# A hybrid decoder's step on one core: two requests' paged values summed on VectorE, the recurrence's outer products formed on TensorE

## The chip, the cores and the metric

One core of a Trainium2 chip runs the whole program. Its engines work side by side, each on its own queue of instructions in order: TensorE (PE) multiplies matrices, VectorE (DVE) and ScalarE (ACT) work elementwise, GpSimd (POOL) does a little elementwise work and issues transfers, SyncE (SP) only issues transfers. Sixteen DMA engines carry these between HBM and the core's SBUF; TensorE writes to PSUM. The metric is the time of one execution on the device, in us.

## The reference, cut to what matters

One layer of a decoder is computed for a prompt of 512 tokens and for eight sample requests with one token each. The mixer has two halves: a gated linear recurrence (HGRN2) and differential attention over a paged cache of 4096 positions per request. Memory cross-attention and a SwiGLU FFN follow. Two pieces of the samples' work are touched here:

```python
# recurrence, per request b and head h (one token): S is 128 x 128
S_new = f[:, None] * S + k[:, None] * v[None, :]
o     = S_new.T @ q
# differential attention over 32 pages of 128 positions, per request
k_past = cache_k[page_table]                 # 32 pages x 128 x 4 heads x 128
v_past = cache_v[page_table]
p = softmax(q . k)                           # two maps
w = p[map 0] - lam * p[map 1]
o = sum over positions of w[position] * v_past[position]      # per head
```

## The kernel before, in words

All data is float32. The prompt's matrix products dominate: each weight row block `raw` of 128 rows is split into a rounded part `hi` (ScalarE, `round_weights`, L655) and a remainder `lo` (VectorE, `remainders`, L669), and each output block takes three products (`block`, L696). A *row of weights* below is one such `hi`/`lo` pair: 12 products of 128x128 by 128x512 in most blocks. `hi` and `lo` lie in rings of three buffers, the raw weights in three of two rows each, all loaded by SyncE (`load_weights`, L617).

The samples' work runs between. `load_keys` and `load_values` (L1099) fetch pages through `stream` (L934), a ring of six buffers of two pages (512 KB), with `gather` (L942) reading page numbers and issuing a DMA per page on SyncE. `sum_values` (L1109) takes, for each request, 32 pages in four visits of eight: each page is multiplied on TensorE by a 128x32 matrix of weights `wt`, four pages side by side in the four groups of 32 columns, accumulated in the PSUM tile `pv`. `value_out` (L1130) then selects each head's row through `pvsel` into `po` and VectorE adds it to `oda_s`.

`sample_recurrence` (L1474) goes through the eight requests: GpSimd loads the state `st`, and loads the request's value row `v` from a copy in HBM (`spill`, `load_row`, L569 to L577) to all 128 partitions as `kv`; ScalarE scales each head's block of `kv` by `k`; VectorE forms `st = f * st + kv`; GpSimd stores it; TensorE multiplies by `q`. GpSimd's queue, in order, holds these triples and other stores.

The order of all instructions is fixed when the program is built. Every piece of work is a generator with a rank; `Weave.run` (L312) always advances the best-ranked one that a model clock (`Clock`, L134) deems ready, and some streams may run VectorE or ScalarE only `LEAD` ahead of TensorE. `pace` (L954) gives a stream its rank only as far as it is behind a straight line over rows of weights: keys over rows 10 to 80 (`KPACE`), values over rows 80 to 150 (`VPACE`). What comes after the samples' attention (`load_rest`, L1872, projections, cross-attention) starts when the values are done; blocks of the FFN that the prompt has passed before the samples reach them are fetched apart (`s_ffn_alone`, L2048). Because every instruction is recorded in `Timed` (L295), all have the line L305 in the profile, and the names of tiles tell them apart.

Of the kernel before, what the change touches and what calls it, by code (L numbers as in the profile page):

```python
# [12 lines left out]
F32 = mybir.dt.float32  # L13
# [365 lines left out]
def decode_step(ctx: ExitStack, tc: tile.TileContext, io: dict):  # L379
# [29 lines left out]
    def slot(s, shape=(P, T), dt=F32):  # L409
        return fp.tile(list(shape), dt, tag="slot", bufs=SLOTS, name=nm(s))  # L410
# [52 lines left out]
    def rsmall(shape, s):  # L463
        return small(shape, s, "r", 2)
# [4 lines left out]
    def row(s):  # L469
        return ring(sp, [P, T], "row", 2, s)  # L470

    def mm(out, a, b, start, stop):
        pe.matmul(out, lhsT=a, rhs=b, start=start, stop=stop)
# [92 lines left out]
        use(pt[:, :P].rearrange("p (g b) -> p g b", b=32))  # L566
        at_give()

    def spill(q, name):  # L569

        d = dp.tile([P, P], F32, name=name)
        pool.dma_start(d, q)
        return d.rearrange("(g b) c -> b g c", b=32)

    def load_row(dst, d, b):

        pool.dma_start(dst.rearrange("p (g c) -> p g c", g=4), d[b].partition_broadcast(P))  # L577


    sizes = [512] * (DFF // 512)  # L580
    sizes.insert(SMALL, DFF % 512)
# [352 lines left out]
    def stream(name):  # L934

        n = streamed[0]
        streamed[0] += 1
        yield lambda: n - KBUFS < done["keys"] + 2 * done["values"] + len(spent) + 2 * done["cmv"] + done["proj"]
        yield clock.next("stream", KBUFS)
        return ring(kp, [P, KPG, T], "stream", KBUFS, name)  # L940

    def gather(which, at, dst):  # L942

        for i, t in enumerate(dst, at):
            if i % PBATCH == 0:
                _, pages[which] = real.values_load_multi_w_load_instructions(
                    ptab[:, which == "cache_v", i : i + PBATCH], [mybir.EngineType.SP], min_val=0, max_val=n_phys - 1,
                    skip_runtime_bounds_check_because="the numbers are clamped to the cache on the chip",
                )
                clock.free["sp"] += 0.53 + 0.03 * PBATCH  # L950
            page = pages[which][i % PBATCH]
# [72 lines left out]
    def sample_softmax():  # L1024
# [71 lines left out]
        dve.tensor_copy(by_quad(wnew), w32.rearrange("p (x b y) -> p x b y", x=2, y=2))  # L1096
        S["wnew"] = True

    def load_values():  # L1099

        yield lambda: len(kts) == NB * nst
        for n in range(NB * NCH):
            pair = []
            for _ in range(2):
                pair.append((yield from stream("cache_v")))
            vts[n] = [t[:, i, :] for t in pair for i in range(KPG)]
            gather("cache_v", 4 * n, vts[n])

    def sum_values():  # L1109
        for n in range(0, NB * NCH, LUMP // 2):  # L1110
            b, s0 = divmod(n, NCH)
            yield lambda: n + LUMP // 2 - 1 in vts and done["soft"] == NB
            if s0 == 0:
                yield from pv_room()
                acc = pvt("pv")
            yield (*(t for i in range(LUMP // 2) for t in vts[n + i]), wts[s0 // 2])
            for s in range(s0, s0 + LUMP // 2):
                w = wts[s // 2].rearrange("p (j b c) -> p j b c", j=2, b=NB)[:, s % 2, b, :]
                for i in range(4):
                    mm(acc[32 * i : 32 * i + 32, :], w, vts[n + s - s0][i], s == 0, s == NCH - 1)  # L1120
            done["values"] = n + LUMP // 2
            if s == NCH - 1:
                yield (acc,)
                pvs = row("pvs")
                act.copy(pvs, acc)
                pv_give()
                weave.add(value_out(b, pvs), 3, "t")
                yield lambda: done["out"] >= b - 1

    def value_out(b, pvs):  # L1130
        yield lambda: done["out"] == b
        yield (pvs,)
        yield from at_room()
        po = att("po")
        for h in range(4):
            mm(po[32 * h : 32 * h + 32, :P], pvsel[:, h, 7 - b : 39 - b], pvs[:, h * P : (h + 1) * P], True, True)
        yield (po,)
        if b == 0:
# [4 lines left out]
        done["out"] = b + 1  # L1143
        if b == NB - 1:
            give(4)
            S["da"] = True

# [326 lines left out]
    def sample_recurrence(sqT, sfT, svq, sgT):  # L1474
        skT = keep([P, 4, 8], "skT")
        lb3 = lb.unsqueeze(2).to_broadcast([P, 4, 8])
        om3 = omlb.unsqueeze(2).to_broadcast([P, 4, 8])
        sig = rsmall([P, 4, 8], "sig")
        yield from sigmoid(sig, skT, sfT)
        dve.scalar_tensor_tensor(skT, skT, BIG, sig, op0=ALU.min, op1=ALU.mult)  # L1480
        dve.tensor_tensor(skT, skT, om3, op=ALU.mult)
        dve.tensor_tensor(sig, sig, om3, op=ALU.mult)
        dve.tensor_tensor(sfT, sig, lb3, op=ALU.add)
        yield
        sig2 = rsmall([P, 4, 8], "sig")
        yield from sigmoid(sig2, sig2, sgT)
        dve.tensor_mul(sgT, sgT, sig2)
        vd = spill(svq, "vd")
        yield from room(2)
        for b in range(NB):  # L1490
            st = slot("st")
            pool.dma_start(st, io["state"][b])
            kv = slot("kv")
# [12 lines left out]
            yield  # L1506
            for h in range(HEADS):
                sl = slice(h * P, (h + 1) * P)
                dve.scalar_tensor_tensor(
                    st[:, sl], st[:, sl], sfT[:, h, b : b + 1], kv[:, sl], op0=ALU.mult, op1=ALU.add  # L1510
                )
            yield
# [359 lines left out]
    def load_rest():  # L1872


        yield lambda: len(vts) == NB * NCH
        yield lambda: "mix" in S or done["values"] >= NB * NCH - LUMP
# [218 lines left out]
    def sample_query(hs):  # L2095
# [20 lines left out]
        yield from new_scores()  # L2116
        S["sn"] = True
        yield lambda: V_FROM in raws
        weave.add(sum_values(), pace(VRANK, "values", NB * NCH, VPACE))
        weave.add(load_values(), 1)  # L2120

    def follower():
# [490 lines left out]
```

## Time and profile before

| | |
|---|---|
| time, median of 3 runs | 1142.68 us (1138.63 to 1144.46) |
| the profiled execution | 1134.85 us, its span 1133.1 us |
| TensorE, share of the span | 95% |
| VectorE | 48% |
| ScalarE | 38% |
| GpSimd | 6% |
| bytes by DMA | 279.75 MB, mean 247 GB/s |

Shares are averages over stages with different limits: the recurrence, keys and the prompt's attention up to some 420 us, the values from 447 to 704 us, the FFN after that. The page's chain of waits names what ended last; a stretch view gives every engine's busy time, the clock granted to TensorE, and the busy share and rate of the DMA engines for that part alone.

### The profile page before, as it was taken

To read this page: it belongs to the slowest core of one execution; us is meant where nothing else is said; L and a number is where in the kernel's file an instruction comes from. 1 tells how busy PE (TensorE), PEld (TensorE's weight loads), DVE (VectorE), ACT (ScalarE), POOL (GpSimd) and SP (SyncE) were. 2 spreads that over 40 slices of the span, in tenths; PEclk is the share of its full clock that TensorE was granted. 3 is DMA by queue.
4 is the path that set the end of the run, shared out by engine and by line. 5 is a ranking of instruction groups with operands and counts; after the bars stand their busy time and mean duration, and the time that the engine had idled before them with its cause. 6 is when DMAs were issued, how large, how long until landed. Compare 5 with 4: busy or idle time off the path is not lost.

```text
span 1133.1 us, 23098 instructions
## 1 busy us (share of the span) xinstructions
PE 1072.3 (95%) x8846; PEld 777.3 (69%) x8846; DVE 546.1 (48%) x1126; ACT 428.3 (38%) x915; POOL 70.4 (6%) x97
## 2 busy tenths in 40 slices
PE   8999799987987889899999999999999999999997
PEld 6777587865665557466666666776577677777776
DVE  6743777534654654444443443453343333443535
ACT  6413443436454556333444332341232221222333
POOL 0000010213101110000300000000000000000002
PEclk9999899988998989999999999999999999999999
DMA  7979665998999995999998799579978982234102
GB/s 255 352 242 324 206 215 174 291 253 259 319 308 278 274 304 169 309 329 332 319 338 285 241 325 343 201 244 359 344 266 291 351 305 75 63 89 129 38 1 75
DMA packets 143376, 279.75 MB, mean 247 GB/s; under 512 B 15281, under 2 KB 20529, under 8 KB 143266
## 3 DMA queue, kind: packets, MB, share of 16 engines
q1 hardware_dynamic: 137970, 264.13, 67.8%
q0 software_dynamic: 4064, 13.05, 6.1%
q8 instruction: 69, 1.13, 0.4%
q10 hardware_dynamic: 1232, 1.11, 0.3%
q14 instruction: 41, 0.34, 0.1%
HBM read 269.35 MB, written 8.88 MB: 246 GB/s over the span
## 4 chain that ended last, share of the span: by engine, by line
PE 81%; DMA 10%; DVE 3%; issue 3%; ACT 1%; SPq 1%; POOL 0%; DVEq 0%; POOLq 0%; ACTq 0%
PE mm L305 56%; DMA cache_k<-cache_k 6%; PE pv L305 5%; PE ks L305 4%; PE sgu L305 2%; PE cs L305 2%; PE sdn L305 1%; DMA kv<-vd 1%; PE ss L305 1%; PE co L305 1%; PE sgm L305 1%; PE pd L305 1%; PE sacc L305 1%; PE oda L305 1%; PE cpv L305 1%
## 5 line engine op out<-in xcount | busy, mean ns | idle before, releaser
L305 DVE TENSOR_TENSOR lo<-raw,hi 128x512 fp32r<-128x512 f32 (+1 forms) x260 | 176.6, 681 | 434.2 <-ACT hi L305 406.1
L305 PE MATMUL mm<-sh,hi 128*128 128x512 f32 (+1 forms) x832 | 339.8, 408 | 4.2 <-ACT sh L305 3.9
L305 ACT CAST hi<-raw 128x512 fp32r<-128x512 f32 (+1 forms) x260 | 157.5, 607 | 490.5 <-PE mm L305 443.3
L305 PE MATMUL mm<-sl,hi 128*128 128x512 f32 (+1 forms) x832 | 324.1, 390 | 0.8 <-DVE sl L305 0.8
L305 PE MATMUL mm<-sh,lo 128*128 128x512 f32 (+1 forms) x832 | 323.0, 388 | 0.0
L305 PEld LDWEIGHTS mm<-sh,hi 128*128 128x128 f32 x832 | 157.2, 189 | 78.6 <-issue 39.0
L305 PEld LDWEIGHTS mm<-sh,lo 128*128 128x128 f32 x832 | 157.5, 189 | 34.0 <-DVE lo L305 0.4
L305 PEld LDWEIGHTS mm<-sl,hi 128*128 128x128 f32 x832 | 157.8, 190 | 28.9 <-DVE sl L305 1.4
L305 PE MATMUL ks<-cache_k,qst 128*32 128x128 f32 x2048 | 72.3, 285 | 16.1 <-DMA cache_k<-cache_k 16.0
L305 PEld LDWEIGHTS ks<-cache_k,qst 128*32 128x32 f32 x2048 | 57.6, 114 | 32.7 <-DMA cache_k<-cache_k 24.0
L305 PE MATMUL pv<-cache_v,wt 128*32 128x512 f32 x512 | 63.4, 608 | 0.0
L305 PE MATMUL mm<-hi,sh 128*128 128x512 f32 x128 | 54.5, 426 | 0.0
L305 PE MATMUL mm<-lo,sh 128*128 128x512 f32 x128 | 50.5, 395 | 0.0
L305 PE MATMUL mm<-hi,sl 128*128 128x512 f32 x128 | 50.5, 394 | 0.0
L305 DVE TENSOR_TENSOR res<-mm,res 128x512 f32<-128x512 f32 (+1 forms) x68 | 42.2, 652 | 9.2 <-PE mm L305 9.2
L305 PEld LDWEIGHTS pv<-cache_v,wt 128*32 128x32 f32 x512 | 14.5, 110 | 31.1 <-issue 22.1
L305 DVE SCALAR_TENSOR_TENSOR lo<-raw,par,hi 128x512 fp32r<-128x512 f32 x16 | 13.2, 826 | 35.1 <-ACT hi L305 35.1
L305 PEld LDWEIGHTS mm<-hi,sh 128*128 128x128 f32 x128 | 24.3, 190 | 7.9 <-issue 3.1
L305 PE MATMUL mm<-hi,mh 128*128 128x512 f32 x64 | 28.5, 446 | 0.9 <-ACT hi L305 0.9
L305 PEld LDWEIGHTS mm<-hi,sl 128*128 128x128 f32 x128 | 24.3, 190 | 5.5
L305 PEld LDWEIGHTS mm<-lo,sh 128*128 128x128 f32 x128 | 24.4, 191 | 4.5 <-issue 0.5
L305 PE MATMUL mm<-lo,mh 128*128 128x512 f32 x64 | 25.2, 394 | 0.2 <-DVE lo L305 0.2
(419 smaller groups left out, 1210.3 us busy)
## 6 DMA issues: line engine op xcount, KB each, us to landing
cache_k<-cache_k SPq DMA_DIRECT2D x256, 256.0 KB, 5.6
cache_v<-cache_v SPq DMA_DIRECT2D x256, 256.0 KB, 4.8
raw<-w_in SPq DMA_DIRECT2D x27, 512.0 KB, 5.1
raw<-w_down SPq DMA_DIRECT2D x22, 512.0 KB, 4.2
raw<-w_gate SPq DMA_DIRECT2D x20, 512.0 KB, 5.0
raw<-w_up SPq DMA_DIRECT2D x20, 512.0 KB, 4.5
cache_mem_k<-cache_mem_k SPq DMA_DIRECT2D x16, 512.0 KB, 6.2
cache_mem_v<-cache_mem_v SPq DMA_DIRECT2D x16, 512.0 KB, 7.4
```

Of the source, the lines that this page charges most:

```text
L305: ins = getattr(self.engine, op)(*a, **k)
```

## The change

Requests 3 and 7 (`BY_DVE`) have their values summed on VectorE: the softmax weights of a request are gathered in `wm` with one column per page and head, and for each page and head one instruction adds value times weight, per position (partition), to an accumulator `va` (128 x 512). Its sum over the 128 positions is then formed by `value_out` with a selection of ones (`ohrow`). The value tiles come in a new order (`vorder`): three of the six other requests' tiles, then one of these. `summed` counts a tile as done only when all before it in that order are, and that count feeds the ring. The values' pace is stretched to rows 80 to 170.

In the recurrence, `k` is transposed once to rows (`krows`); a row mask (`mine`) leaves, for request b, its four heads' rows (`km`); `vcols` holds each head's `v` in its own columns and rows, zero elsewhere. One product `km` by `vcols` in plain fp32 gives the four heads' outer products in PSUM, which VectorE reads as `kv`. The copy of `v` in HBM and the eight loads of it are gone.

```diff
+BY_DVE = (3, 7)
+EVERY = 3
-VPACE = (80, 150)
+VPACE = (80, 170)
...
-        yield lambda: n - KBUFS < done["keys"] + 2 * done["values"] + len(spent) + 2 * done["cmv"] + done["proj"]
+        yield lambda: n - KBUFS < done["keys"] + done["values"] + len(spent) + 2 * done["cmv"] + done["proj"]
...
+    while by_pe or by_dve:
+        vorder += by_pe[:EVERY] + by_dve[:1]
+        del by_pe[:EVERY], by_dve[:1]
...
     def sum_values():
...
+        if BY_DVE:
+            weave.add(sum_values_dve(), 5, "d")
+        for b in range(NB):
+            if b in BY_DVE:
+                continue
...
+    def sum_values_dve():
...
+            acc = slot("va")
+            for s in range(nst):
+                yield lambda: b * nst + s in vts
+                v = vts[b * nst + s]
+                yield tuple(v)
+                for i in range(KPG):
+                    for h in range(HEADS):
+                        c = slice(h * P, (h + 1) * P)
+                        k = 4 * (KPG * s + i) + h
+                        if s + i == 0:
+                            dve.tensor_scalar(acc[:, c], v[i][:, c], wm[:, k : k + 1], None, op0=ALU.mult)
+                        else:
+                            dve.scalar_tensor_tensor(
+                                acc[:, c], v[i][:, c], wm[:, k : k + 1], acc[:, c], op0=ALU.mult, op1=ALU.add
+                            )
+                    yield 0.0
+                summed(b * nst + s)
...
-        vd = spill(svq, "vd")
         yield from room(2)
...
+        yield from s_tr(padded, lambda pt: dve.tensor_copy(krows, pt.rearrange("p g b -> p (g b)")))
+        for h in range(HEADS):
+            r = slice(32 * h, 32 * h + 32)
+            act.copy(vcols[r, h * P : (h + 1) * P], svq[r])
...
-            load_row(kv, vd, b)
-            yield
-            for h in range(HEADS):
-                sl = slice(h * P, (h + 1) * P)
-                act.activation(kv[:, sl], kv[:, sl], AF.Copy, scale=skT[:, h, b : b + 1])
+            km = quadt("km")
+            dve.tensor_scalar(km, krows, mine[:, b : b + 1], None, op0=ALU.mult)
...
+            yield from at_room()
+            kv = att("kv")
+            mm(kv, km, vcols, True, True)
+            yield (kv, st)
```

On TensorE, at the recurrence's first request, the program before goes on like this (`mm` is a block of the prompt's projections, `so` the state times `q`, `ks` the scores of eight pages of keys):

```order
L305 MATMUL mm_3068<-sl_202,hi_3306 128x512
L305 MATMUL mm_3068<-sh_201,lo_3340 128x512
L305 MATMUL so_3423<-st_3268,qm_3386 32x128 x4
L305 MATMUL mm_3136<-sh_201,hi_3306 128x512
L305 MATMUL mm_3136<-sl_202,hi_3306 128x512
L305 MATMUL mm_3136<-sh_201,lo_3340 128x512
L305 MATMUL mm_3147<-sh_201,hi_3306 128x512
L305 MATMUL mm_3147<-sl_202,hi_3306 128x512
L305 MATMUL mm_3147<-sh_201,lo_3340 128x512
L305 MATMUL ks_3416<-cache_k_3193,qst_588 32x128 x8
L305 MATMUL ks_3416<-cache_k_3230,qst_588 32x128 x8
L305 MATMUL ks_3416<-cache_k_3344,qst_588 32x128 x8
```

In the changed program the same place reads:

```order
L307 MATMUL mm_3136<-sl_202,hi_3315 128x512
L307 MATMUL mm_3136<-sh_201,lo_3349 128x512
L307 MATMUL ks_3421<-cache_k_3193,qst_588 32x128 x8
L307 MATMUL ks_3421<-cache_k_3230,qst_588 32x128 x8
L307 MATMUL ks_3421<-cache_k_3353,qst_588 32x128 x8
L307 MATMUL ks_3421<-cache_k_3356,qst_588 32x128 x8
L307 MATMUL kv_3490<-vcols_3267,km_3381 128x512
L307 MATMUL mm_3147<-sh_201,hi_3315 128x512
L307 MATMUL mm_3147<-sl_202,hi_3315 128x512
L307 MATMUL mm_3147<-sh_201,lo_3349 128x512
L307 MATMUL mm_3257<-sh_201,hi_3315 128x512
L307 MATMUL mm_3257<-sl_202,hi_3315 128x512
```

One product `kv` stands behind the keys' scores, and `so` of that request comes 12 products of the prompt later.

On VectorE, at the prompt's memory queries (`cq`, `cql`) and the splits of memory values and keys (`mvl`, `kl`), the program before has:

```order
L305 SCALAR_TENSOR_TENSOR lo_6879<-raw_6657,par,hi_6841 128x512
L305 TENSOR_TENSOR cq_6885<-mm_6550,rbc 128x512
L305 TENSOR_TENSOR cql_6867<-cq_6829,cqh_6866 128x512
L305 TENSOR_TENSOR mvl_6870<-mv_5163,mvh_6869 128x512
L305 SCALAR_TENSOR_TENSOR lo_6908<-raw_6657,par,hi_6898 128x512
L305 TENSOR_TENSOR kl_6873<-mkT_4511,kh_6872 128x512
L305 TENSOR_TENSOR kl_6888<-mkT_4513,kh_6887 128x512
L305 TENSOR_TENSOR cql_6911<-cq_6885,cqh_6910 128x512
L305 TENSOR_TENSOR mvl_6903<-mv_5202,mvh_6902 128x512
L305 TENSOR_TENSOR mvl_6941<-mv_5791,mvh_6940 128x512
L305 TENSOR_TENSOR mvl_6989<-mv_5802,mvh_6988 128x512
L305 TENSOR_REDUCE cmx_6948<-cs_6947 128x2
```

The changed program has there:

```order
L307 SCALAR_TENSOR_TENSOR lo_6957<-raw_6742,par,hi_6945 128x512
L307 TENSOR_TENSOR mvl_6937<-mv_5710,mvh_6936 128x512
L307 TENSOR_TENSOR cql_6952<-cq_6893,cqh_6951 128x512
L307 SCALAR_TENSOR_TENSOR va_5965<-cache_v_6919,wm_5960,va_5965 128x128 x8
L307 SCALAR_TENSOR_TENSOR lo_6999<-raw_6793,par,hi_6975 128x512
L307 TENSOR_TENSOR cql_6963<-cq_6902,cqh_6962 128x512
L307 TENSOR_TENSOR mvl_6979<-mv_5922,mvh_6978 128x512
L307 TENSOR_TENSOR oda_s<-oda_s,po_6981 128x128
L307 TENSOR_REDUCE cmx_7007<-cs_7006 128x2
L307 TENSOR_SCALAR cmx_7007<-cmx_7007 128x2
L307 SCALAR_TENSOR_TENSOR lo_7047<-raw_6793,par,hi_7037 128x512
L307 TENSOR_TENSOR mvl_7023<-mv_5955,mvh_7022 128x512
```

Eight sums of one value tile (two pages, four heads) stand between two remainders `lo`, in a queue that otherwise holds the same kinds of instructions.

## Rows read from the trace of the kernel before

**Rows 1.** The page's head: span, busy time of each engine.
```profile
span 1133.1 us, 23098 instructions
PE 1072.3 (95%) x8846; PEld 777.3 (69%) x8846; DVE 546.1 (48%) x1126; ACT 428.3 (38%) x915; POOL 70.4 (6%) x97
```

**Rows 2.** Stretches: length, busy us, granted clock, DMA share, GB/s.
```profile
0.00:220.00 220.00, 203.91 (x2926) 162.70 (x2927) 139.65 (x320) 92.17 (x205) 17.52 (x31) 0.96 0.77 259
220.00:420.00 200.00, 169.92 (x1702) 121.63 (x1701) 103.12 (x249) 96.74 (x237) 34.15 (x46) 0.92 0.96 281
300.00:320.00 20.00, 18.92 (x215) 14.47 (x214) 13.18 (x37) 10.02 (x25) 2.89 (x5) 1.00 1.01 370
447.00:704.00 257.00, 252.64 (x1422) 163.16 (x1414) 110.32 (x191) 99.41 (x199) 11.29 (x10) 0.99 0.91 310
704.00:1050.00 346.00, 345.56 (x2281) 249.13 (x2279) 135.72 (x248) 93.97 (x178) 0.62 (x2) 1.00 0.65 227
```

**Rows 3.** Stretches of low DMA rate, the same columns.
```profile
223.00:230.00 7.00, 7.00 (x88) 5.92 (x88) 0.89 (x2) 0.50 (x1) 0.00 (x0) 1.00 0.92 71
240.00:247.00 7.00, 7.00 (x75) 5.82 (x68) 1.63 (x3) 1.24 (x2) 0.00 (x0) 0.94 0.99 86
258.00:262.50 4.50, 1.04 (x40) 0.77 (x30) 0.69 (x1) 1.58 (x2) 0.00 (x0) 0.88 1.05 93
292.00:297.50 5.50, 4.82 (x33) 3.73 (x34) 2.10 (x5) 2.19 (x4) 0.00 (x0) 1.00 1.04 125
322.00:326.50 4.50, 3.43 (x14) 2.47 (x14) 1.76 (x4) 4.47 (x14) 0.00 (x0) 1.00 0.90 68
348.50:355.50 7.00, 6.07 (x59) 4.32 (x57) 4.56 (x12) 3.82 (x13) 0.00 (x0) 1.00 0.93 94
372.00:378.00 6.00, 5.98 (x49) 3.83 (x38) 3.95 (x12) 2.90 (x7) 0.82 (x2) 1.00 0.87 82
393.00:400.50 7.50, 5.62 (x33) 3.18 (x33) 2.53 (x7) 0.00 (x0) 0.00 (x0) 1.00 0.86 89
```

**Rows 4.** Timeline of GpSimd: start, us, instruction, idle before it.
```profile
222.08 0.76 POOL L305 DMA_DIRECT2D kv<-vd  x1 [5.36 <-DMA vd<-svq]
...
287.63 0.75 POOL L305 DMA_DIRECT2D kv<-vd  x1
307.41 0.55 POOL L305 DMA_DIRECT2D out_hg_sample<-st  x1 [19.03 <-DVE st L305]
...
388.50 0.76 POOL L305 DMA_DIRECT2D kv<-vd  x1
```

**Rows 5.** DMA issues: count, KB each, median us to landing.
```profile
st<-state POOLq DMA_DIRECT2D x8, 256.0 KB, 6.1
kv<-vd POOLq DMA_DIRECT2D x8, 256.0 KB, 11.4
```

**Rows 6.** Waits from 220 to 420 us: total us, times, longest.
```profile
PEld ks L305 <- DMA cache_k<-cache_k: 22.9, 23, 6.3
ACT kv L305 <- DMA kv<-vd: 21.1, 3, 9.3
```

**Rows 7.** The chain of waits, one sum over partitions: start, us, what.
```profile
665.87 0.86 PE ss L305 x2
```

**Rows 8.** The chain, a visit to the values and products of the prompt.
```profile
694.75 1.85 PE pv L305 x16
696.60 5.71 PE mm L305 x24
...
974.06 16.54 PE mm L305 x72
```

**Rows 9.** The values' group on the page: busy us, mean ns.
```profile
L305 PE MATMUL pv<-cache_v,wt 128*32 128x512 f32 x512 | 63.4, 608 | 0.0
```

**Rows 10.** VectorE on the recurrent state: one run, and its group.
```profile
410.64 1.13 DVE L305 SCALAR_TENSOR_TENSOR st<-st,scols,kv 128x128 f32<-128x128 f32 x4
L305 DVE SCALAR_TENSOR_TENSOR st<-st,scols,kv 128x128 f32<-128x128 f32 x32 | 12.2, 443 | 0.0
```

**Rows 11.** A cast and its remainder in time; the remainders' group, 447 to 704 us.
```profile
668.61 0.62 ACT L305 CAST hi<-raw 128x512 fp32r<-128x512 f32 x1 [0.49 <-PE mm L305]
669.26 0.69 DVE L305 TENSOR_TENSOR lo<-raw,hi 128x512 fp32r<-128x512 f32 x1 [2.89 <-ACT hi L305]
L305 DVE TENSOR_TENSOR lo<-raw,hi 128x512 fp32r<-128x512 f32 x40 | 27.7, 692 | 81.0 <-ACT hi L305 76.6 <-PE mm L305 4.4
```

More of the change, by code (lines that the diff above doesn't have):

```diff
@@ L567, in s_tr @@
         at_give()
[L569 to L577, printed above, removed]
     sizes = [512] * (DFF // 512)
@@ L944, in gather @@
         for i, t in enumerate(dst, at):
+            key = which, at // NPG in BY_DVE and which == "cache_v"
             if i % PBATCH == 0:
-                _, pages[which] = real.values_load_multi_w_load_instructions(
+                _, pages[key] = real.values_load_multi_w_load_instructions(
                     ptab[:, which == "cache_v", i : i + PBATCH], [mybir.EngineType.SP], min_val=0, max_val=n_phys - 1,
@@ L950, in gather @@
                 clock.free["sp"] += 0.53 + 0.03 * PBATCH
-            page = pages[which][i % PBATCH]
+            page = pages[key][i % PBATCH]
             sync.dma_start(t, ckv[which][bass.ds(page, 1), :, :].rearrange("o p c -> (o p) c"))
@@ L1097, in sample_softmax @@
         S["wnew"] = True
+    by_pe = [b * nst + n for b in range(NB) if b not in BY_DVE for n in range(nst)]
+    by_dve = [b * nst + n for b in BY_DVE for n in range(nst)]
+    vorder, vsummed = [], set()
+    while by_pe or by_dve:
+        vorder += by_pe[:EVERY] + by_dve[:1]
+        del by_pe[:EVERY], by_dve[:1]
     def load_values():
         yield lambda: len(kts) == NB * nst
[L1102 to L1107, printed above, removed]
@@ L1109, in sum_values @@
-    def sum_values():
[L1110 to L1128, printed above, removed]
@@ L1130, in value_out, with summed, ticket @@
-    def value_out(b, pvs):
-        yield lambda: done["out"] == b
+        for n in vorder:
+            t = yield from stream("cache_v")
+            vts[n] = [t[:, i, :] for i in range(KPG)]
+            gather("cache_v", KPG * n, vts[n])
+    def summed(n):
+        vsummed.add(n)
+        while done["values"] < len(vorder) and vorder[done["values"]] in vsummed:
+            done["values"] += 1
+    def ticket():
+        tickets[0] += 1
+        return tickets[0] - 1
+    tickets = [0]
+    def sum_values():
+        if BY_DVE:
[3 more added lines that the diff above has]
+                continue
+            for s0 in range(0, nst, LUMP):
+                yield lambda: b * nst + s0 + LUMP - 1 in vts and done["soft"] == NB
+                if s0 == 0:
+                    yield from pv_room()
+                    acc = pvt("pv")
+                yield (*(t for i in range(LUMP) for t in vts[b * nst + s0 + i]), wts[s0 // 4])
+                for s in range(s0, s0 + LUMP, 2):
+                    w = wts[s // 4].rearrange("p (j b c) -> p j b c", j=2, b=NB)[:, s % 4 // 2, b, :]
+                    for i in range(4):
+                        mm(
+                            acc[32 * i : 32 * i + 32, :], w, vts[b * nst + s + i // 2][i % 2],
+                            s == 0, s == nst - 2,
+                        )
+                for i in range(LUMP):
+                    summed(b * nst + s0 + i)
+            yield (acc,)
+            pvs = row("pvs")
+            act.copy(pvs, acc)
+            pv_give()
+            n = ticket()
+            weave.add(value_out(n, b, pvs, pvsel[:, :, 7 - b : 39 - b]), 3, "t")
+            yield lambda: done["out"] >= n - 1
@@ new lines, in sum_values_dve @@
+    def sum_values_dve():
+        yield lambda: done["soft"] == NB
+        yield (wts[3],)
+        yield from room(1)
+        wms = slot("wm", (P, len(BY_DVE), P))
+        yield from room(1)
+        for wm, b in zip([wms[:, i, :] for i in range(len(BY_DVE))], BY_DVE):
+            for i, w in enumerate(wts):
+                w5 = w.rearrange("p (j b c m) -> p j b c m", j=2, b=NB, m=2)[:, :, b]
+                dve.tensor_tensor(
+                    wm[:, 32 * i : 32 * i + 32].rearrange("p (j c) -> p j c", j=2),
+                    w5[:, :, :, 0], w5[:, :, :, 1], op=ALU.add,
+                )
+            acc = slot("va")
[12 more added lines that the diff above has]
+                                acc[:, c], v[i][:, c], wm[:, k : k + 1], acc[:, c], op0=ALU.mult, op1=ALU.add
+                            )
+                    yield 0.0
+                summed(b * nst + s)
+            n = ticket()
+            weave.add(value_out(n, b, acc, ohrow[:, 7 - b : 39 - b].unsqueeze(1).to_broadcast([P, HEADS, 32])), 3, "t")
+            yield lambda: done["out"] > n
+        give(2)
@@ L1132, in value_out @@
+    def value_out(n, b, pvs, sel):
+        yield lambda: done["out"] == n
         yield (pvs,)
@@ L1487, in sample_recurrence @@
         dve.tensor_mul(sgT, sgT, sig2)
-        vd = spill(svq, "vd")
         yield from room(2)
+        krows, vcols = quadt("krows", tag="rows", bufs=1), slot("vcols")
+        pool.memset(vcols, 0.0)
+        padded, mine = quadt("padded"), rsmall([P, 32], "mine")
+        dve.memset(padded, 0.0)
+        dve.tensor_copy(padded.rearrange("p (h b) -> p h b", h=4)[:, :, :NB], skT)
+        dve.tensor_reduce(mine, ident.rearrange("p (h b) -> p b h", h=4), axis=AX.X, op=ALU.add)
+        yield
+        yield from s_tr(padded, lambda pt: dve.tensor_copy(krows, pt.rearrange("p g b -> p (g b)")))
+        for h in range(HEADS):
+            r = slice(32 * h, 32 * h + 32)
+            act.copy(vcols[r, h * P : (h + 1) * P], svq[r])
+        yield
         for b in range(NB):
@@ L1511, in sample_recurrence @@
                 )
+            at_give()
             yield
@@ L1872, in load_rest @@
     def load_rest():
-        yield lambda: len(vts) == NB * NCH
-        yield lambda: "mix" in S or done["values"] >= NB * NCH - LUMP
+        yield lambda: len(vts) == len(vorder)
+        yield lambda: "mix" in S or done["values"] >= len(vorder) - 2 * LUMP
         S["mixed"] = KT // 2 if "mix" in S else 0
@@ L2118, in sample_query @@
         yield lambda: V_FROM in raws
-        weave.add(sum_values(), pace(VRANK, "values", NB * NCH, VPACE))
+        weave.add(sum_values(), pace(VRANK, "values", NB * nst, VPACE))
         weave.add(load_values(), 1)
```

9 lines of the change are left out of this document (4 added, 5 removed).

## Prediction

> **What bounds the kernel now.** I read the page's head first, then the busy time by stretch, then the waits of the slow stretch, and the chain of waits last. TensorE is busy for 95% of the span of 1133.1 us, VectorE for 48% [rows 1], so the reader should ask where TensorE is not busy, and at which clock it ran. The stretches answer [rows 2]. From 447 to 1050 us TensorE is busy for 598.2 of 603 us: whatever it no longer has to do there comes off the end one for one. From 220 to 420 us it is idle for 30.1 of 200 us and was granted 0.92 of full speed, a mean over the 1.2 and 2.4 GHz levels, while the DMA engines are 96% busy and yet move only 281 GB/s; 20 us inside it, from 300 to 320, show 370 GB/s and 1.1 us of idle TensorE. So this stretch is short of transfers, and something makes transfers slow.
>
> What that is stands in the rates [rows 3]: in eight short windows, 49 us together, the DMA engines are 86 to 105% busy and move 68 to 125 GB/s. GpSimd's queue issues a triple per request there (store the state of the last request, load the next, load the broadcast value row kv), and each window opens a few us after a kv load, as after the first, fourth and last of the eight [rows 4]. The two partners alone don't do it: 300 to 320 us holds a store of a state and 370 GB/s. A kv load takes 11.4 us to land, a state of the same size 6.1 [rows 5]. The waits agree: TensorE sits idle for the keys, and ScalarE, in order, stood 21.1 us before three kv scalings, with the casts of the prompt's weights and the softmax of the prompt's heads queued behind it [rows 6].
>
> **Recurrence, 220 to 420 us.** Removed: eight kv loads, 32 kv scalings on ScalarE, the spill of v. At the 370 GB/s of [rows 2] the eight windows' bytes (rate times length, summed: 4.3 MB) would have taken 12 of their 49 us, so some 37 us of DMA time come back, besides 2.1 MB that need not move. TensorE gains work: eight products of 128x128 by 128x512 in plain fp32. The nearest row is the sum of squares over partitions, the same shape: 0.86 us [rows 7]; with 0.2 us for the change between kinds of product (below), 8 x 1.06 = 8.5 us. VectorE gets eight row scalings and reads kv from PSUM, at most 5 us on an engine that is half idle (103 of 200 us).
> How much of the 30.1 us comes back is the open size. Upper end: all of the clock (169.9 x 0.92 = 156.3 us of work) and idle as from 300 to 320 us (5.4%): (156.3 + 8.5) / 0.946 = 174 us, 26 gained. Lower end: the stalls stay, because they belong to the softmax chains of the prompt's heads, and the products come on top: 8.5 lost. I take half of the clock back and the idle share of 0 to 220 us (16.1 of 220, 7.3%), the stretch ahead without kv loads: (163.1 + 8.5) / 0.927 = 185 us, so **15 us gained**.
> On the price of kv a page of the Trainium skill says otherwise. "DMA: Bandwidth & Descriptors" (Anatomy of one DMA) fits a transfer of GpSimd's queue by about 2 us fixed plus its bytes at 436 GB/s; an estimate from it is 0.6 us of data per kv load, 5 us for all eight. The trace disagrees, with 11.4 us to landing and the windows above, which the page's fit doesn't know.
>
> **Values, from 447 us.** Two of eight requests leave TensorE. A visit to the values is 16 records, 1.85 us, and there are 32; eight go. Their way back costs too: 24 products of the prompt between two visits take 5.71 us, and 72 without a visit 16.54, that is 5.51 for 24 [rows 8]: 0.2 us per visit. 8 x 2.05 = **16.4 us gained**; by the group's busy time, a quarter of 63.4 us [rows 9], it would be 15.9. The selection of the outputs stays at eight rounds.
> VectorE gets 256 instructions of 128x128. The same form on the recurrent state took 1.13 us for four in a row, 0.283 each; the mean with the gaps and contended ones counted is 0.443 [rows 10]. So 72 us, at most 113, into a stretch where it was busy for 110 of 257: 75 to 91%. It has room on average; the question is order. TensorE's next weights need the remainder `lo`, one of these per row of weights, in order on VectorE, and the new order puts up to eight sums (2.3 us) between two of them. The cover: a cast waits for TensorE to finish with a buffer of three, as in its row, and `lo` follows (0.62 and 0.69 us) [rows 11]; two rows of 12 products (2.75 us each) are then still ahead, which leaves some 4 us. A burst of 2.3 fits, unless it meets residual sums and splits: the order has one place with seven of these at 0.69 around the eight sums, 7.1 us between two `lo`. I charge **4 us** for a few such places; between nothing and the slower rival below.
> What is queued behind a late sum: a buffer of the six comes free late, SyncE's next page waits, and the weights behind it. The buffers for weights hold three loads of two rows, some 16 us of work, so this is covered.
>
> **The end.** The span of the values goes from 70 to 90 rows of weights, so the sample's later steps start later. In the new order four blocks of the FFN instead of three are fetched apart for the sample: 24 more loads of 256 KB, 6.3 MB, less four loads of 512 KB for w_out, which half passes with the prompt's. TensorE's columns stay the same (32 products of 256 for 64 of 128). The extra 4.2 MB are 11 us of DMA at 370 GB/s, behind 346 us in which the DMA is 65% busy [rows 2]. In both orders the sample's last weight product stands 273 products of the prompt ahead of the end, so it is not late: nothing.
>
> **Sum.** -15 - 16.4 + 4 = -27.4. The profiled execution took 1134.85 us around its span of 1133.1 and would come to 1107; the three timed runs have a median of 1142.68 (1138.63 to 1144.46), and I set the change against that: **1115 us**.
>
> **Rivals.**
> Only the values pay: kv's slow windows are hidden or replaced by other waits, so the stretch stays within -2 to +4 us around even (idle time absorbs the products). 1142.7 - 12 = about 1130. For it: TensorE also waits there for softmax results and for its own issue; against it: the rows of rates. By the page's fit the stretch would gain at most its 5 us, the same case. Chance 0.18.
> Everything comes back: the upper end of the recurrence and no late `lo`: -26 - 16.4 = 1100. For it: from 420 us on TensorE runs without a gap at full clock. Chance 0.17.
> VectorE becomes the bound and the kernel **slower**: in the values' stretch `lo` is late behind the sums. Price: up to 2.3 us for each of 32 tiles, 73 us with no cover; the change turns into a loss from about 1 us of stall per tile (31.4 / 32). At half the full price: -31.4 + 37 = +6, 1149; contended forms at 0.443 would give 1160. For it: the place with 7.1 us; against it: mean busy share under 80%, and `lo` waits for ScalarE now, not for VectorE (81 us of idle before it [rows 11]). Chance 0.06.
> The sample's chain is late: the fourth separate block arrives when the prompt has ended, or the values drag the weights: the gain shrinks to within the noise, about 1140. Against it: the unchanged order at the end. Chance 0.05.
> The forecast's own case, 1106 to 1124: chance 0.54.
>
> **Numbers.** A difference under 0.5% (5.7 us) can't be told from none. Faster: 0.54 + 0.17 + 0.17 of the 0.18; same: the rest of that and 0.05; slower: 0.06. The range takes in the upper end and most of the case in which only the values pay: 1097 to 1133.
>
> **What would show it.** Right: from 220 us on no window under 130 GB/s for 5 us, no kv wait on ScalarE, the first values product about 15 us earlier than 447 us; then values visits of 1.85 us, 24 of them, with VectorE near 75% busy and `lo` still waiting for ScalarE. Wrong: TensorE idle on `lo` in the values' stretch for more than 10 us, or low rates that remain with kv gone, or waits for FFN weights after 1000 us.

## The result, and the profile after

The changed kernel takes 1094.41 us, the median of four runs (1090.33 to 1097.08), against 1140.66 us (1133.83 to 1144.46) of the kernel before on the same chip: a ratio of 0.9603 [0.9558, 0.9648]. The forecast was 1115 us, 1097 to 1133. The sign was right, and the kernel was faster than the range allowed.

The two profiled executions are 37.8 us apart (1134.85 and 1097.08 us), the medians 46.3: the traced execution of before was among its short ones, and the traced one of after the longest of its four. Everything read from the two traces therefore has to add up to 37.8.

The page of after, first its head, to be read beside [rows 1]:

```profile
span 1095.3 us, 23060 instructions
PE 1051.1 (96%) x8672; PEld 770.9 (70%) x8672; DVE 620.9 (57%) x1404; ACT 417.1 (38%) x884; POOL 63.4 (6%) x89
```

The stretches of both kernels, cut at the first product of the values (446.7 us before, 409.3 after) and behind the last. The columns are those of [rows 2]. First the kernel before:

```profile
220.00:446.70 226.70, 196.62 (x1846) 141.97 (x1845) 117.42 (x290) 116.82 (x285) 35.23 (x48) 0.93 0.92 272
446.70:704.60 257.90, 253.54 (x1425) 163.75 (x1425) 110.32 (x191) 99.71 (x199) 11.29 (x10) 0.99 0.91 309
704.60:1133.10 428.50, 418.21 (x2657) 308.86 (x2656) 178.76 (x325) 119.57 (x227) 6.37 (x8) 0.99 0.55 190
```

And the changed kernel:

```profile
220.00:409.30 189.30, 181.80 (x1835) 132.56 (x1835) 115.11 (x293) 107.82 (x254) 24.03 (x32) 0.97 0.85 294
409.30:721.30 312.00, 303.38 (x1570) 214.04 (x1570) 208.54 (x493) 115.53 (x227) 15.57 (x19) 0.99 0.83 281
721.30:1095.30 374.00, 363.95 (x2357) 263.61 (x2349) 155.90 (x295) 101.48 (x198) 6.38 (x8) 0.99 0.62 216
```

In the recurrence's stretch TensorE's idle time fell from 30.1 to 7.5 us and its granted clock rose from 0.93 to 0.97. The first product of the values comes 37.4 us earlier, but not all of that is gain. By then 864 instead of 924 of the prompt's products have run: 60 x 0.23 = 13.8 us of work (0.23 from the last of [rows 8]) has moved behind it, and some small products have moved ahead. What both come to can be read from rec_only (below), which has the changed recurrence and the values as before. It too has run 864 of the prompt's products by its first value, and these are its stretches from there to its end:

```profile
407.50:681.50 274.00, 268.67 (x1483) 174.22 (x1484) 114.32 (x196) 102.07 (x203) 15.57 (x19) 1.00 0.89 305
681.50:1107.20 425.70, 415.57 (x2634) 307.09 (x2626) 179.10 (x327) 119.19 (x225) 6.38 (x8) 0.99 0.53 187
```

That is 699.7 us, 13.3 more than the 686.4 of before. So the recurrence gained 37.4 - 13.3 = 24.1 us in the changed kernel. From the first value to the end the changed kernel takes 686.0 us, so the values and what follows gained 699.7 - 686.0 = 13.7 us.

The low rates of [rows 3] are gone. These are the three lowest windows of 7 us that after has between 220 and 409 us (columns as above):

```profile
388.00:395.00 7.00, 4.54 (x17) 2.15 (x16) 3.91 (x12) 6.88 (x19) 0.00 (x0) 0.87 0.24 78
395.00:402.00 7.00, 7.00 (x39) 5.92 (x41) 3.71 (x8) 4.06 (x8) 0.00 (x0) 0.88 0.49 150
402.00:409.00 7.00, 7.00 (x50) 5.26 (x45) 1.41 (x6) 3.35 (x7) 0.76 (x2) 1.00 0.02 5
```

They move little while the DMA engines are mostly idle (shares of 0.24, 0.49 and 0.02), so little is asked for; in [rows 3] the engines were 86 to 105% busy at such rates. In every such window of after in which the engines are over 90% busy they move 290 GB/s or more. Two of the three lie under the 130 GB/s that the forecast named as a sign, which shows that the rate and the share must be read together. The waits of that stretch, after, beside [rows 6], say the same: the keys are late by 8.0 us in place of 22.9, and VectorE has a small new wait for the product kv.

```profile
PEld ks L307 <- DMA cache_k<-cache_k: 8.0, 12, 1.5
DVE st L307 <- PE kv L307: 5.0, 3, 3.2
```

The groups of the values, on the page of after, beside [rows 9]:

```profile
L307 DVE SCALAR_TENSOR_TENSOR va<-cache_v,wm,va 128x128 f32<-128x128 f32 x248 | 75.0, 373 | 10.7 <-DMA cache_v<-cache_v 10.7
L307 PE MATMUL pv<-cache_v,wt 128*32 128x512 f32 x384 | 48.7, 599 | 0.1
```

TensorE's part fell by 14.7 us, and VectorE's sums take 75.0 us, near the first value of the forecast (72). VectorE is busy 208.54 of 312 us there, 67%. One thing in this stretch was not forecast. The timeline of VectorE in after (start, us, what), two groups of eight sums:

```profile
513.28 2.17 DVE L307 SCALAR_TENSOR_TENSOR va<-cache_v,wm,va 128x128 f32<-128x128 f32 x8
...
520.99 9.33 DVE L307 SCALAR_TENSOR_TENSOR va<-cache_v,wm,va 128x128 f32<-128x128 f32 x8
```

And GpSimd's at the same time, where it restores the prompt's residual from its two halves:

```profile
520.72 9.18 POOL L307 TENSOR_TENSOR res<-sh,sl 128x512 f32<-128x512 f32 x7 [104.75 <-PE cs L307]
```

The eight sums take 9.33 us instead of 2.17, while GpSimd's seven additions run (in after_again, too, one group takes 9.33 us), and the softmax of the memory and a `lo` stand behind them. The Trainium skill ("SBUF — State Buffer", SBUF: two separate sides) says that VectorE with two inputs from SBUF and a GpSimd operation that reads SBUF share one pair of ports, held for the whole instruction; this trace agrees as to the stall, 9.33 for 2.17 us.

The longest wait of TensorE in the stretch, 4.15 us, is for that softmax (cpt is its transpose):

```profile
533.20 1.30 PE L307 MATMUL cpt<-con,cp 128*128 128x128 f32 x4 [4.15 <-ACT cp L307]
```

The next, 3.08 us, comes from VectorE's order. These are lines of the timelines of VectorE and of TensorE in after:

```profile
414.60 0.69 DVE L307 TENSOR_TENSOR lo<-raw,hi 128x512 fp32r<-128x512 f32 x1 [0.98 <-ACT hi L307]
422.32 2.24 DVE L307 SCALAR_TENSOR_TENSOR va<-cache_v,wm,va 128x128 f32<-128x128 f32 x8 [7.03 <-DMA cache_v<-cache_v]
...
425.82 0.50 PE L307 MATMUL mm<-sh,lo 128*128 128x512 f32 x1 [3.08 <-DVE lo L307]
```

VectorE stood 7.03 us before sums whose page of values had not landed (in the window from 402 us above next to nothing had been asked for), with the next `lo` behind them.

### The profile page after: what moved, and what is told of

Its sections match the earlier page's. It is cut to its first block, busy times and chain, and to the rows that moved or that the text cites. A ratio compares the mean times of both kernels' runs of the same rounds, so it can differ in the third digit from the quotient of the medians.

```text
span 1095.3 us, 23060 instructions
## 1 busy us (share of the span) xinstructions
PE 1051.1 (96%) x8672; PEld 770.9 (70%) x8672; DVE 620.9 (57%) x1404; ACT 417.1 (38%) x884; POOL 63.4 (6%) x89
## 4 chain that ended last, share of the span: by engine, by line
PE 85%; DVE 6%; DMA 4%; issue 2%; ACT 2%; SPq 1%; DVEq 0%; ACTq 0%
PE mm L307 60%; PE ks L307 5%; PE pv L307 4%; PE sgu L307 2%; DMA cache_k<-cache_k 2%; PE cs L307 2%; PE sdn L307 1%; PE sgm L307 1%; DMA cache_v<-cache_v 1%; PE ss L307 1%; DVE va L307 1%; SPq L307 1%; DVE lo L307 1%; PE co L307 1%; PE oda L307 1%
## 5 line engine op out<-in xcount | busy, mean ns | idle before, releaser
L307 DVE TENSOR_TENSOR lo<-raw,hi 128x512 fp32r<-128x512 f32 (+1 forms) x260 | 179.4, 693 | 360.6 <-ACT hi L307 329.2
L307 DVE SCALAR_TENSOR_TENSOR va<-cache_v,wm,va 128x128 f32<-128x128 f32 x248 | 75.0, 373 | 10.7 <-DMA cache_v<-cache_v 10.7
L307 PE MATMUL ks<-cache_k,qst 128*32 128x128 f32 x2048 | 66.0, 276 | 3.8 <-DMA cache_k<-cache_k 3.7
L307 PEld LDWEIGHTS ks<-cache_k,qst 128*32 128x32 f32 x2048 | 55.1, 110 | 17.7 <-DMA cache_k<-cache_k 9.5
L307 PE MATMUL pv<-cache_v,wt 128*32 128x512 f32 x384 | 48.7, 599 | 0.1
L307 PEld LDWEIGHTS pv<-cache_v,wt 128*32 128x32 f32 x384 | 10.5, 109 | 24.4 <-issue 20.4
L307 PE MATMUL mm<-hi,ml 128*128 128x512 f32 x64 | 25.7, 402 | 0.0
```

The costliest lines, as they stand in the source:

```text
L307: ins = getattr(self.engine, op)(*a, **k)
```

## The experiments

Two theories on the recurrence came out of this. Theory 1: the eight kv loads themselves, while in flight, choke the DMA engines; what the change won is their absence. Rival 1: ScalarE, which stood in order before late kv scalings, was what held TensorE up. Theory 2, on the values: they gain what TensorE's visits cost, less what GpSimd's collision takes.

**Both halves, and the loads.** The changed kernel again, each half alone, and before with a single kv load (the first request's v serves all eight, so the outer products of seven are made from a wrong v).

```diff
 after, recurrence only (rec_only)
-BY_DVE = (3, 7)
+BY_DVE = ()
-VPACE = (80, 170)
+VPACE = (80, 150)
 val_only: after with before's recurrence (not shown)
 before, one load (one_load)
...
+            if b == 0:
+                load_row(kv0, vd, 0)
-            load_row(kv, vd, b)
-                act.activation(kv[:, sl], kv[:, sl], AF.Copy, ...)
+                act.activation(kv[:, sl], kv0[:, sl], AF.Copy, ...)
```

after_again. 

> The changed kernel itself, for a narrower interval beside the others. If the ratio of 0.960 was helped by a slow pair of runs of the kernel before, it comes out nearer the profiles' difference (37.8 of 1134.85 us), 0.967; otherwise 0.955 to 0.965.

rec_only. 

> Only the recurrence's half of the change: all eight requests' values stay on TensorE, paced over rows 80 to 150 as before. Theory 1 (the slow kv loads held back the whole stretch from 220 to 420 us): the first values product comes some 24 us earlier, after as many products of the prompt; 25 us faster, ratio 0.978. Rival (the forecast's size: half of that comes back, the products on TensorE eat the rest): 15 us, ratio 0.987.

val_only. 

> Only the values' half: requests 3 and 7 on VectorE, pace 80 to 170, kv loaded to all partitions as before. Theory 1: the halves add, the values give the 16.4 us of TensorE less some 4 us of stalls: 12 us faster, ratio 0.989. Rival (the values give more than TensorE's visits, since the stretched pace also relieves the DMA): 25 us or more, ratio 0.978.

one_load. 

> The kernel before with one kv load instead of eight: the first request's value row is scaled for all eight requests (so the other seven states come from a wrong v); ScalarE's scalings, VectorE's updates, state loads and stores stay. Theory 1: no stretch under 130 GB/s for 5 us any more except after that one load, and without TensorE's extra 8.5 us this gains at least as much as the recurrence's half, 25 to 33 us, ratio 0.971 to 0.978. Rival (the low rates come from the states' loads and stores, or from the stretch's own softmax chains): under 10 us, ratio above 0.991.

Measured, against 1140.97 us of before: after again 1094.13 us, 0.9598 [0.9559, 0.9636]; rec_only 1109.20, 0.9712 [0.9673, 0.9751]; val_only 1120.44, 0.9829 [0.978, 0.9879]; one_load 1096.59, 0.9617 [0.9578, 0.9655]. The first result stands. The recurrence alone brings 31.8 us in these medians (by the spans of the profiles 1133.1 - 1107.2 = 25.9), more than either case that was expected and twice what the prediction had for it. The loads alone cost 44 us, more than the 25 to 33 expected: with seven of eight gone, before is as fast as the whole change. The stretch from 220 us to the first value, in one_load:

```profile
220.00:408.70 188.70, 181.84 (x1849) 135.86 (x1847) 117.14 (x289) 117.55 (x285) 29.53 (x41) 0.98 0.93 314
```

The values' half, from its first value (445.0 us) to its end, in val_only:

```profile
445.00:737.80 292.80, 287.98 (x1509) 202.98 (x1508) 205.07 (x490) 113.23 (x223) 11.23 (x10) 0.99 0.83 285
737.80:1114.80 377.00, 367.12 (x2389) 264.30 (x2381) 155.25 (x291) 101.90 (x200) 6.37 (x8) 0.99 0.62 220
```

That is 669.8 us against 686.4 in before, 16.6 less, and TensorE is busy 655.1 instead of 671.75 us, 16.65 less: all that TensorE saves comes off the end. Both expected sizes missed: the 12 us left 4 for stalls that don't show here, and the 25 wanted a gain beyond TensorE's work that doesn't show either (20.5 us in the medians, 18.3 in the spans). Here GpSimd's additions came in shorter runs, and no group of eight sums took more than 4.32 us.

**Loads, or ScalarE's place in the order?** unused_loads is one_load with all eight loads issued again, into a buffer that nothing reads. kv_spread and kv_2k change how a load reads: kv_spread takes as many 512-byte pieces from distinct places of the value cache (it is not v that it reads), kv_2k stores a request's v as one 2-KB row, so that each partition reads one piece. restore_dve is the changed kernel with the eight residual additions on VectorE.

```diff
 unused_loads
...
+            load_row(slot("kvx"), vd, b)
 kv_spread
...
-            load_row(kv, vd, b)
+            pool.dma_start(kv.rearrange("p (g c) -> p g c", g=4),
+                io["cache_v"][4 * b : 4 * b + 4].rearrange("g (p c) -> p g c", p=P)[:, :, :P])
 kv_2k
...
-        d = dp.tile([P, P], F32, name=name)
-        pool.dma_start(d, q)
+        d = dp.tile([32, 4 * P], F32, name=name)
+        for g in range(4):
+            pool.dma_start(d[:, g * P : (g + 1) * P], q[32 * g : 32 * g + 32])
...
-        pool.dma_start(dst.rearrange("p (g c) -> p g c", g=4), d[b].partition_broadcast(P))
+        pool.dma_start(dst, d[b].partition_broadcast(P))
 restore_dve
...
-                pool.tensor_tensor(res[j], f32(xh[j]), f32(xl[j]), op=ALU.add)
+                dve.tensor_tensor(res[j], f32(xh[j]), f32(xl[j]), op=ALU.add)
```

unused_loads. 

> As one_load (one kv load is scaled for all eight requests), but the eight loads of the kernel before are issued again, at the same places, into buffers that nothing reads: ScalarE never waits for one. Theory 1 (the loads slow down every other transfer while they are in flight): the time goes back most of the way to the kernel before, 1125 to 1140 us. Rival (ScalarE, in order, waiting for kv held up the casts and the softmax): it stays within 10 us of one_load, about 1100.

kv_spread. 

> The kernel before, but kv is loaded from the paged values instead of the broadcast row: again 256 KB in pieces of 512 bytes, but each partition reads addresses of its own (so the states come from a wrong v). Theory 1a (128 partitions reading one and the same row of HBM is what is slow): kv lands in about 6 us, as the states do, no windows under 130 GB/s, 1098 to 1110 us. Rival 1b (pieces of 512 bytes, or GpSimd's queue, are slow): no change, about 1141, landing near 11 us.

kv_2k. 

> The kernel before, with the copy of v laid out so that a request's row of 2 KB is one piece: 128 partitions still read the same address, in pieces of 2 KB instead of four of 512 bytes. Theory 1a (the same address): no gain to speak of, 1130 to 1141 us. Rival 1b (the pieces' size): kv lands in about 6 us, 1098 to 1110.

restore_dve. 

> The changed kernel with the eight additions that restore the residual moved from GpSimd to VectorE. In the changed kernel's profile eight sums took 9.3 us instead of 2.2 while GpSimd ran these additions, and TensorE then sat idle for 4.9 us between 500 and 550. Theory 2 (the two engines held each other up there): no such run of sums, 4 to 5 us faster than the changed kernel, 1089 to 1091 us, although VectorE gets 5.5 us more work. Rival (TensorE's stall there comes from the number of VectorE's instructions): no change or slower, 1094 to 1100.

Measured, against 1134.79 us: unused_loads 1144.14, 1.0074 [1.0045, 1.0104]; kv_spread 1095.41, 0.9634 [0.9591, 0.9677]; kv_2k 1098.11, 0.9648 [0.9604, 0.9693]; restore_dve 1095.72, 0.9637 [0.9591, 0.9682]. In unused_loads ScalarE has no eight loads to wait for, and all the loss is back and a little more (it is 0.7% slower than before), so rival 1 falls. Its DMA issues (count, KB each, median us to landing), three windows, and its wait for keys from 220 to 450 us:

```profile
kvx<-vd POOLq DMA_DIRECT2D x8, 256.0 KB, 12.2
...
220.00:227.00 7.00, 7.00 (x88) 5.64 (x87) 1.92 (x4) 1.24 (x2) 0.92 (x2) 1.00 0.93 83
227.00:234.00 7.00, 6.08 (x60) 4.30 (x58) 3.09 (x8) 2.89 (x7) 1.84 (x3) 1.00 0.88 57
...
318.00:325.00 7.00, 5.38 (x81) 3.81 (x77) 4.79 (x17) 1.79 (x7) 0.00 (x0) 1.00 0.97 141
...
PEld ks L305 <- DMA cache_k<-cache_k: 40.5, 24, 7.2
```

A load that nobody waits for lands in 12.2 us. In the first window two loads are in flight, the one that is used and the first unused one, and the second window takes in the end of these and the start of the next; behind a single one, issued at 315 us, the rate is 141 GB/s at a share of 0.97. TensorE pays at the keys, where PE's weight loads wait 40.5 us in place of 22.9 [rows 6]. But neither the small pieces alone (kv_spread) nor the same bytes read by 128 partitions alone (kv_2k) are slow, so both explanations of it fell.

restore_dve shows half of theory 2. Its stretch from 500 to 550 us, and its values' stretch:

```profile
500.00:550.00 50.00, 49.15 (x288) 32.13 (x278) 42.90 (x110) 22.89 (x56) 0.00 (x0) 1.00 0.92 323
406.70:719.20 312.50, 306.17 (x1567) 214.01 (x1570) 204.71 (x500) 116.00 (x227) 5.23 (x11) 0.99 0.82 281
```

The same 50 us in after:

```profile
500.00:550.00 50.00, 45.15 (x251) 29.41 (x243) 45.10 (x94) 22.55 (x55) 10.71 (x9) 0.97 0.83 281
```

The collision is gone, and with it 4 us of idle TensorE in those 50 us. Yet the whole stretch lasts as long (312.5 against 312.0), and the kernel is not faster than after. So the collision is shown, a gain from ending it is not.

**Distance, and a better kernel.** The pieces of v lie 16 KB apart in before (32 rows of 512 bytes). kv_near puts them 528 bytes apart and leaves all else, but for four writes of v in place of one. best_2k is val_only with kv_2k's rows: values on VectorE, outer products as before. three_2k adds a third request.

```diff
 kv_near
...
+        d = dp.tile([32, 4, P + 4], F32, name=name)
+            pool.dma_start(d[:, g, :P], q[32 * g : 32 * g + 32])
+        return d[:, :, :P]
 three_2k
-BY_DVE = (3, 7)
-EVERY = 3
+BY_DVE = (2, 4, 7)
+EVERY = 2
```

best_2k. 

> The values' half of the change, with the recurrence's outer products left on ScalarE and VectorE as before, but the spilled v stored so that one request's row is one 2-KB piece, loaded by one request per partition. If the two gains are separate (the load's slow pieces in the recurrence, TensorE's visits in the values), it takes kv_2k's ratio 0.965 and the 16.6 us of the values: 0.949 to 0.953, about 1082 us, some 12 us under the changed kernel, since TensorE has none of its eight products. Rival: ScalarE's and VectorE's passes on the outer products, or VectorE's sums next to GpSimd's additions, eat the gain again: 0.960 or more, no better than the changed kernel.

three_2k. 

> The same kernel with a third request's values on VectorE (requests 2, 4 and 7, a tile of one of them behind every second of the others'). One more request takes 4 visits of 1.85 us and their loads from TensorE (about 8 us) and gives VectorE 128 more operations of 0.34 us (44 us) in a stretch of about 300 in which it was busy 65%. If TensorE still sets the pace: 0.942 to 0.946, about 7 us under the kernel with two. Rival: VectorE's sums now hold up the splits that TensorE waits for, and the gain is lost: equal to the kernel with two or slower.

kv_near. 

> The kernel before with one thing changed: the four 512-byte pieces of a request's v row lie 528 bytes apart in memory instead of 16 KB, still as four pieces for each of the 128 partitions. Theory (many small reads of the same few bytes are slow): as slow as before, ratio 0.99 to 1.01, kv landing in 11 us or more. Rival (the distance of 16 KB between the pieces is what is slow): as fast as with 2-KB pieces, 0.960 to 0.970.

Measured, against 1139.35 us: kv_near 1102.73, 0.9678 [0.9642, 0.9715]; best_2k 1083.25, 0.9530 [0.9494, 0.9566]; three_2k 1090.28, 0.9580 [0.9545, 0.9616]. The theory that kv_near was to confirm fell: many small reads of the same bytes are not slow when the pieces lie side by side. best_2k is 11 us below the changed kernel's median of another call; by the ratios, 0.9530 against 0.9598, it is 8. three_2k is 7 us above best_2k in the same call, so the third request gains nothing. The values' stretches, best_2k:

```profile
410.40:703.20 292.80, 288.59 (x1509) 202.96 (x1508) 204.82 (x489) 113.05 (x223) 11.23 (x10) 0.99 0.83 286
```

and three_2k:

```profile
416.10:698.40 282.30, 270.12 (x1379) 189.38 (x1378) 212.38 (x547) 109.05 (x217) 11.31 (x10) 0.98 0.81 278
```

With three requests TensorE stands idle for 12.2 us there instead of 4.2, although VectorE is busy for only 75%. These 8 us are what four visits fewer were to save, so the rival's case came; but the traced execution of three_2k was the longest of its six (1098.78 us against a median of 1090.28), so they may overstate it. Its two longest waits of TensorE in this stretch (total us, times, longest):

```profile
PE cpt L307 <- ACT cp L307: 5.9, 2, 5.5
PE mm L307 <- DVE sl L307: 2.1, 1, 2.1
```

The first is again the softmax of the memory, whose reduction on VectorE stands behind eight sums that took 6.29 us beside six of GpSimd's additions. Waits of 1.5 us for the remainder cpl on VectorE and 1.6 us for pages follow; in best_2k, softmax waits of 3.8 us are nearly all.

**Which distance?** Three controls write v in four pieces as kv_near does, with 32, 8 and 33 rows of 512 bytes between a row's pieces: 16, 4 and 16.5 KB.

```diff
 kv_far33 (32 for 33 in kv_far; in kv_4k 8, and 8 rows are written)
...
+        d = dp.tile([4, 33, P], F32, name=name)
+        for g in range(4):
+            pool.dma_start(d[g, :32], q[32 * g : 32 * g + 32])
+        return d.rearrange("g b c -> b g c")
```

kv_far. 

> A control for kv_near: v is spilled by the same four writes, but to rows whose four 512-byte pieces lie 16 KB apart, as in the kernel before. Theory (the distance between the pieces is what makes the loads slow): as slow as the kernel before, ratio 0.99 to 1.01, kv landing in 11 us or more, stretches below 130 GB/s behind the loads. Rival (the one 64-KB write of the spill, not the distance, was slow to be read back): 0.965 to 0.970 as kv_near, landing near 8.8 us.

kv_4k. 

> The same control with the pieces 4 KB apart, at 8 rows of 512 bytes in place of 32. If any distance that keeps the four pieces from lying side by side is slow: 0.99 to 1.01. If only the 16 KB is: 0.965 to 0.970. Between them, about 0.98, if the loss grows with the distance.

kv_far33. 

> The same control with the pieces 16.5 KB apart (33 rows of 512 bytes). If the exact distance of 16 KB is what is slow (pieces that fall onto the same place of the memory): 0.965 to 0.970. If any distance as long as that is: 0.99 to 1.01.

Measured, against 1139.20 us: kv_far 1140.77, 1.0023 [0.998, 1.0066]; kv_4k 1106.55, 0.9724 [0.9647, 0.9801]; kv_far33 1096.55, 0.9627 [0.9561, 0.9694]. The landing of the kv loads, and the first 80 us of the recurrence, in kv_far:

```profile
DMA to landing us min/median/max: 9.7/11.6/12.9
...
220.00:300.00 80.00, 63.39 (x629) 45.26 (x628) 30.43 (x51) 31.14 (x60) 18.81 (x18) 0.87 0.91 247
```

and in kv_far33, whose v has one more unused row in each block of 32:

```profile
DMA to landing us min/median/max: 4.6/7.8/8.9
...
220.00:300.00 80.00, 78.31 (x862) 59.85 (x864) 47.41 (x91) 44.02 (x91) 21.20 (x22) 1.00 0.95 329
```

With the same instructions, bytes and pieces, 512 bytes more between the pieces turn 247 into 329 GB/s, let TensorE run 78.3 instead of 63.4 of 80 us at full clock, and take 43 us off the kernel. Of the distances tried only the exact 16 KB is slow. 4 KB is within the errors of kv_near, and may cost a little. Other distances, 8 or 32 KB say, were not run, and why 16 KB is slow is not shown.

## Why the prediction was wrong

**What bounds the kernel: right.** The stretch from 220 us was short of transfers, the kv loads made them slow, and unused_loads shows it without ScalarE's waits.

**Recurrence, 15 us: the step that failed.** It measured 24.1 us in the changed kernel's trace and 25.9 by the spans of rec_only, near the upper end of 26 that stood in the text, and 32 in the medians of rec_only. The step reads "I take half of the clock back and the idle share of 0 to 220". The clock was nearly right (0.97 granted, 0.96 assumed). The idle share was not: 7.5 of 189.3 us is 4.0%, where 7.3% was taken. In the sum as it stands, (163.1 + 8.5) / 0.927 = 185 becomes 171.6 / 0.96 = 179, 6 us less, and with the measured clock 177; the last us is not told apart. A stretch of other work, 0 to 220 us, was taken as the model for this one.

A better row was not to be had from the trace of before. From 300 to 320 us [rows 2] TensorE idled 5.4%, but a kv load was issued inside it:

```profile
316.74 0.76 POOL L305 DMA_DIRECT2D kv<-vd  x1
```

And in the eight gaps between the latest landing of a kv load (13.4 us after its issue) and the next issue, 91 us together, TensorE stood idle for 7.5 us, 8.2%. So the idle time is not confined to the loads' own flights, and only a run without the loads gives the share: 3.6% in one_load.

The other 8 us are in the baseline: 46.3 by the medians, 37.8 by the two traces. The forecast took differences read from an execution of 1134.85 us off a median of 1142.68, as if both were the same case. In the calls of the experiments the runs of before lie 12 to 15 us apart, those of one_load and kv_2k 5 to 8. But kv_near and three_2k, whose loads are not slow, spread over 14 us as well, and unused_loads, whose loads are, over 9; so that the slow loads are what varies is not shown.

The eight products were charged 8.5 us. In the trace of after one takes 0.86 to 1.06 us, which was right. rec_only, which has them, is 12.6 us behind one_load in the same call, and by the ratios 10 behind kv_far33, which has cheap loads in their place. So the products, with what prepares them, cost some 8 to 13 us, and they were not needed.

**On the page.** The forecast set the fit of the Trainium skill's page "DMA: Bandwidth & Descriptors" against 11.4 us to landing and left the gap unexplained. The same page of the Trainium skill (Latency and other measured facts) has a rule that points the right way: rows at large powers of two apart are slow in HBM, and padding cures that. Its figures don't cover this case: they are for copies from the sync and scalar queues, 207 GB/s at a pitch of 512 KiB between partitions and 103 at 4 MiB, restored by 4 KiB of padding and not by 192 bytes. Here GpSimd's loads were slow at 16 KB between pieces that all partitions share, and 512 bytes cured it. The page calls the mechanism an inference; these runs show the address distance, not the mechanism.

**Values, 16.4 us: right.** val_only has 16.6. The visits stayed at 1.85 us, there are 24, and VectorE's work is 75.0 us where 72 was taken. VectorE's share was not right: 75 to 91% divides by a stretch of some 245 us, although the wider pace spreads the values over 312, where it came to 67%.

**Late `lo`, 4 us: near in size by luck, wrong in reason.** The values and what follows gained 13.7 us in the changed kernel, 2.7 less than 16.4; in val_only, with the same sums on VectorE, they gained 16.6 and the stalls cost nothing. The two waits found in after are 3.08 us for a `lo` that stood behind sums waiting for their page, and 4.15 us behind GpSimd's additions; the seven instructions around eight sums that the forecast feared cost nothing that the waits show. It named what waits for a late sum, not what a sum itself waits for: on an engine in order, a page that is late holds up every `lo` behind its sums. Since restore_dve won nothing, the collision's share is not shown to reach the end. The halves alone add up to 52 us in the medians of their call and both together to 47; by the traces about half of these 5 us is the 16.6 that became 13.7, and the rest stays open.

**The end: right.** From 736 to 1050 us TensorE never waits in after, and the sample's fourth separate block is not late. **Rivals:** "everything comes back" (1100 us, 0.17) was the nearest, without its condition of no stall. In the rival of a slower kernel, 1160 does not follow from 0.443: half of 256 x 0.443 is 57 us, which gives 1168; nothing turned on it. VectorE was never the bound with two requests; with three its sums begin to hold TensorE up.

## What to carry to other kernels

When a small load lands late and DMA engines are busy at a low rate, look at the distance between the pieces it reads before redesigning what uses it: one unused row of padding gave 43 us, nearly as much as the whole change. Price a stall that goes from a run in which its cause is taken out, where one can be had, not from another stretch: one_load gave the idle share that no row of before shows. And when a change mixes two gains, take the halves apart: here the values were worth keeping and the products were not.

## What the runs showed of the hardware

- Loads of 256 KB in 512-byte pieces, the same four pieces for all 128 partitions, land in 11.4 to 12.2 us and press all queues to 68 to 141 GB/s (57 with two in flight) if the pieces are 16 KB apart; 8.6 to 8.8 us at 4 KB or 528 bytes, 7.8 at 16.5 KB or as one 2-KB piece (before, unused_loads and kv_far; kv_4k, kv_near; kv_far33, kv_2k).
- Eight sums of 128x128 on VectorE took 9.33 instead of 2.17 us beside seven of GpSimd's additions of 128x512, and at most 4.32 in the shorter overlaps of val_only and best_2k.
